# Norm factors of both layers loaded ahead of layer 0, and keys of two latent heads made by one matmul

## The chip, the core and the metric

The kernel runs on one core of a Trainium2 chip. Five engines work side by side on it, each with its own instruction stream that it works off in order: TensorE (PE in the profile; its weight loads are PEld), VectorE (DVE), ScalarE (ACT), GpSimd (POOL) and SyncE (SP), which here only issues DMAs. The metric is the time of one execution on the device in microseconds, as a median of several runs.

## The reference

Two layers of an encoder over 512 tokens of width 1024. Each layer projects its input once, and three kinds of attention share the result: six latent heads (A), six dilated heads (B) and four grouped-query heads over two key heads (C). Then come an output projection, a normalisation, a SwiGLU network of width 2816 and another normalisation. What the change touches are A's keys and values and C's norm factors:

```python
for l in range(DEPTH):                       # DEPTH = 2
    h = x @ w_in[l]
    ckv = rms_norm(h[..., 256:384], mla_kv_norm[l])
    # A: 128 latent values of a token give 6 heads x (64 key + 64 value) columns
    kva = (ckv @ mla_w_ukv[l]).reshape(B, S, 6, 64 + 64)
    ka = concatenate([kva[..., :64], rope(k_rope) broadcast to 6 heads])
    va = kva[..., 64:]
    out_a = dense_attention(qa, ka, va, 96 ** -0.5)
    out_b = dilated_mixture(...)
    # C: 4 query heads and 2 key heads of 64, each normalised and rotated
    qc = rms_norm(qc, gqa_q_norm[l]);  kc = rms_norm(kc, gqa_k_norm[l])
    out_c = dense_attention(axial_rope(qc), axial_rope(kc), vc, 64 ** -0.5)
    x = layer_norm(ALPHA * x + concatenate([out_a, out_b, out_c]) @ w_out[l])
    x = layer_norm(ALPHA * x + (silu(x @ w_gate[l]) * (x @ w_up[l])) @ w_down[l])
```

All inputs are float32; `gqa_q_norm` and `gqa_k_norm` are vectors of 64 values for each layer.

## The kernel before

**Numbers.** Every float32 operand of a projection is split into a high and a low part, and a product is made by three matmuls: high by high, high by low, low by high (`mm3`, L162 to L167; in the profile they are L165, L166 and L167). A weight is brought in by `wload` (L142 to L157): SP issues a DMA into a raw buffer (L150; two such buffers take turns), ScalarE copies it rounded into `whi` (L152), and VectorE or GpSimd subtracts to get `wlo` (L156).

**Order of the work.** A layer first projects the values of the dilated heads and then runs its 16 attention heads one after another in units of one head and one tile of 128 queries (`attend`): scores (L241), the row's minimum and the exponential, the reciprocal of the sum (L255), the scaling of the row by it on GpSimd (`pl`, L256), transposition on TensorE (`ptr`, L264) with the split into PTh and PTl (L271, L272), and the product with the values (`po`, L282 and L283), three and four units later. Six dilated heads come first, then four grouped-query heads, then six latent heads. The other projections of the layer are cut into steps that a table of units (`W`, L33) spreads between the attention units, so that TensorE has work while a softmax runs. A scheduler finally orders the instructions of every engine when the kernel is built, by its own estimate of times; on the chip each engine works its list off in order. After attention come the rest of the output projection, the normalisation and the feed-forward network, which fill more than half of the time.

**Grouped-query norm factors.** At each layer's head a tile `gg` of 128 partitions by 6 heads by 64 is filled by six DMAs (L406), four of `gqa_q_norm` and two of `gqa_k_norm`; each repeats one vector of 64 on all partitions. VectorE then scales the first four by -1/8 (L407). `gg` has one buffer, so layer 1's loads can't start before layer 0 has used it for the last time (L426 in `evac_g2`).

**Latent heads.** `latent_qv` loads the two halves of `w_uq` and `w_ukv` as whole rows of 768 columns, in the order head, key or value, column; it makes the queries (`uq`) and, with the value columns of all heads as a moving operand of 384 columns, the values (`uv`). `mla_T(h)` runs once a head, at the units that `W['mT']` names: it transposes the queries (`tT`), and makes the keys by one `mm3` with 64 columns of weights and 512 tokens as moving operand (`kT`, 64 partitions of a PSUM bank). ScalarE and VectorE write the high and low part into a tile of the head, whose partitions 64 to 95 get the rotated keys by a DMA. These tiles share four buffers with the queries; the `kT`, `uv`, `uq` and projection products share two PSUM banks (`ps_mm`).

Of the kernel before, what the change touches and what calls it, by code (L numbers as in the profile page):

```python
# [10 lines left out]
F32 = mybir.dt.float32  # L11
F32R = mybir.dt.float32r
AF = mybir.ActivationFunctionType
ALU = mybir.AluOpType
# [67 lines left out]
def encoder(ctx: ExitStack, tc, x, w_in, mla_q_norm, mla_kv_norm, w_uq, w_ukv, gqa_q_norm, gqa_k_norm, rel_bias,  # L82
# [30 lines left out]
    def bank(pl, name):  # L113
        return pl.tile([P, 512], F32, tag="b", name=name)
# [24 lines left out]
             "m": ((pmix, "m"), (pmix, "m"))}  # L139
    turn = {"raw": 0}  # L140

    def wload(src, shape, lo, ring="w", raw="w"):  # L142

        n = shape[1] * shape[2]
        if raw == "wd":
            turn["raw"] += 1
            raw = "wwdd"[turn["raw"] % 4]
        (hp, ht), (lp, lt) = parts[ring]
        r = raws[raw][0].tile([P, 1024], F32, tag=raws[raw][1], name="wraw")
        nc.sync.dma_start(r[:, :n].rearrange("p (a c) -> p a c", a=shape[1]), src)  # L150
        h = hp.tile([P, 1024], F32R, tag=ht, name="whi")
        A.copy(h[:, :n], r[:, :n])  # L152
        o = lp.tile([P, 1024], F32R, tag=lt, name="wlo")
        step = n // 2 if lo is G and SPLIT else n
        for c in range(0, n, step):
            lo.tensor_tensor(o[:, c:c + step], r[:, c:c + step], h[:, c:c + step].bitcast(F32), op=ALU.subtract)  # L156
        return (h[:, :n].rearrange("p (a c) -> p a c", a=shape[1]), o[:, :n].rearrange("p (a c) -> p a c", a=shape[1]))  # L157

    def krows(w, k0, nk, c0, c1):
        return w[k0 * P:(k0 + nk) * P, c0:c1].rearrange("(k p) c -> p k c", p=P)  # L160
# [232 lines left out]
    for l in range(DEPTH):  # L393
# [3 lines left out]
        if l == 0:  # L397
            nc.sync.dma_start(tab[:, P:], tabs[:, P:])
            for i in range(DEPTH):
                nc.sync.dma_start(gm[:, i, 0:2], mla_q_norm[i].rearrange("(k p) -> p k", p=P))  # L400
                nc.sync.dma_start(gm[:, i, 2:3], mla_kv_norm[i].rearrange("(k p) -> p k", p=P))

        gg = pgg.tile([P, 6, HD], F32, tag="gg", name="gg")
        for i in range(6):
            src = (gqa_q_norm if i < 4 else gqa_k_norm)[l]
            nc.sync.dma_start(gg[:, i], src.unsqueeze(0).to_broadcast([P, HD]))  # L406
        V.tensor_scalar(gg[:, 0:4], gg[:, 0:4], -(HD ** -0.5), None, op0=ALU.mult)  # L407

        g2, gv, gkk = {}, {}, []

# [112 lines left out]
        def mla_T(h):  # L523
            assert ("q", h // 3) in told
            to_T(lambda t: tq[0][:, t, h, :], 96, mqk[h])
            yield
            pb = bank(ps_mm, "kT")
            wk = [w[:, 0, h * P:h * P + HD] for w in wkv[0]]
            r = pqk.tile([P, 2, T], F32R, tag="q", name="kT")
            nc.sync.dma_start(r[HD:96].bitcast(F32), krT[0][:32].bitcast(F32))  # L530
            mm3(pb[:HD], wk, (latT[2][:, 0], latT[2][:, 1]), True, True)
            A.copy(r[:HD, 0], pb[:HD])
            V.tensor_tensor(r[:HD, 1], pb[:HD], r[:HD, 0].bitcast(F32), op=ALU.subtract)
            mqk[h].append(r)
            yield

        def dil_qk(pair):
# [36 lines left out]
        def latent_qv():  # L574
            q = pxt.tile([P, NT, 6, 96], F32, tag="x", name="tq")
            tq.append(q)
            wq = [wload(krows(w_uq[l], 0, 2, 288 * c, 288 * c + 288), (P, 2, 288), LO['uq']) for c in range(2)]
            wkv.append(wload(krows(w_ukv[l], 0, 1, 0, 768), (P, 1, 768), LO['kv']))
            yield
            for c in range(2):  # L580
                h, o = wq[c]
                for t in range(NT):
                    pb = bank(ps_mm, "uq")[:, :288]
                    ts = slice(t * P, (t + 1) * P)
                    for k in range(2):
                        mm3(pb, (latT[k][:, 0, ts], latT[k][:, 1, ts]), (h[:, k], o[:, k]), k == 0, k == 1)
                    A.copy(q[:, t, 3 * c:3 * c + 3, :], pb.rearrange("p (h c) -> p h c", h=3))
                    yield
                tm = ppl.tile([P, T], F32, tag="l", name="qrt")[:, :384].rearrange("p (t h c) -> p t h c", t=NT, h=3)
                rope32(q[:, :, 3 * c:3 * c + 3, 64:96], 3, tm)  # L590
                told.append(("q", c))
            h, o = (w[:, 0].rearrange("p (h c) -> p h c", h=6)[:, :, HD:] for w in wkv[0])
            for t in range(NT):
                pb = bank(ps_mm, "uv")[:, :6 * HD]
                ts = slice(t * P, (t + 1) * P)
                mm3(pb, (latT[2][:, 0, ts], latT[2][:, 1, ts]), (h, o), True, True)
                vt = pv_sb.tile([P, 6, 2, HD], F32R, tag="v", name="mv")
                split_v(vt, pb.rearrange("p (a c) -> p a c", a=6))
                mv_.append(vt)
                yield  # L600
# [53 lines left out]


        latT, krT, tq, mv_, wkv, dts, told = [], [], [], [], [], {}, []
        gqk, dqk, mqk = ([[] for _ in range(n)] for n in (2, 3, 6))
        heads = []
        for h in range(6):
# [205 lines left out]
```

## Time and profile before

| | before |
|---|---|
| median of three runs | 1281.85 us (1281.53 to 1283.26) |
| profiled execution, its own time | 1282.31 us |
| its span, first to last instruction | 1280.5 us |
| TensorE busy | 98% of the span |
| VectorE / ScalarE / GpSimd busy | 54% / 42% / 25% |
| mean granted clock of TensorE | 0.994 |
| mean DMA traffic | 96 GB/s |

A row of the timeline gives the start of an instruction, how long it took, the engine, the line of the kernel, the operation, the tile written, the tiles read and the shape. In square brackets stands how long the engine had been idle before it and what ended that. Matmuls are pipelined, so the distance of two starts tells more of TensorE than the length of one. The granted clock is a share of TensorE's full speed: 1.00 is 2.4 GHz, 0.50 is 1.2 GHz.

### The profile page before, as it was taken

How to read it: one execution, taken by the hardware profiler on the slowest of the kernel's cores; microseconds unless marked ns; L12 is line 12 of the kernel's file. 1: busy time of each engine (PE TensorE's matmuls, PEld its weight loads, DVE VectorE, ACT ScalarE, POOL GpSimd, SP SyncE). 2: the span in 40 equal slices, each digit the busy share in tenths (PEclk: the TensorE clock that was granted, in tenths of full speed). 3: DMA queues.
4: the chain of work that ended last, by engine and by line, in shares of the span. 5: the costliest groups of instructions: out<-in, count | busy, mean ns of one | idle time of the engine just before them, and what ended most of it. 6: DMA issues, size and time to landing. Idle time of an engine off the chain costs nothing.

```text
span 1280.5 us, 16743 instructions
## 1 busy us (share of the span) xinstructions
PE 1250.1 (98%) x6352; PEld 1062.5 (83%) x6352; DVE 687.7 (54%) x1138; ACT 543.6 (42%) x955; POOL 324.6 (25%) x344
## 2 busy tenths in 40 slices
PE   8999899999999999999999998999999999999997
PEld 7888788889888888888898897888988888888885
DVE  4377997684333333332664889966843332333346
ACT  4465786544222212222245668855342221222222
POOL 0445475661000000000245456655500000000004
PEclk9999899999999999999999999999999999999999
DMA  5623210324333233332425231114243333333223
GB/s 179 188 67 87 87 34 13 120 69 130 99 99 97 89 96 98 99 99 99 148 78 147 84 103 48 28 30 134 77 115 99 99 99 99 99 99 98 92 96 110
DMA packets 140552, 122.57 MB, mean 96 GB/s; under 512 B 6924, under 2 KB 114572, under 8 KB 140472
## 3 DMA queue, kind: packets, MB, share of 16 engines
q1 hardware_dynamic: 140460, 121.48, 32.0%
q8 instruction: 50, 0.82, 0.3%
q14 instruction: 30, 0.25, 0.1%
q10 hardware_dynamic: 12, 0.02, 0.0%
HBM read 114.65 MB, written 2.12 MB: 91 GB/s over the span
## 4 chain that ended last, share of the span: by engine, by line
PE 80%; DVE 8%; DMA 4%; ACT 3%; POOL 2%; issue 2%; SPq 0%; DVEq 0%; POOLq 0%; ACTq 0%
PE gate L165 6%; PE down L167 6%; PE down L166 6%; PE up L167 6%; PE down L165 6%; PE up L165 6%; PE up L166 6%; PE gate L167 6%; PE gate L166 6%; PE sc L241 4%; PE ptr L264 3%; PE po L283 2%; PE po L282 2%; PE tp L166 1%; PE tp L165 1%
## 5 line engine op out<-in xcount | busy, mean ns | idle before, releaser
L152 ACT CAST whi<-wraw 128x1024 fp32r<-128x1024 f32 (+3 forms) x202 | 205.6, 1020 | 550.6 <-PE gate L166 149.3
L156 DVE TENSOR_TENSOR wlo<-wraw,whi 128x1024 fp32r<-128x1024 f32 (+3 forms) x170 | 208.2, 1226 | 319.7 <-ACT whi L152 315.7
L191 POOL TENSOR_TENSOR rstd<-mv,eps_l 128x1 f32<-128x1 f32 x16 | 5.7, 357 | 680.8 <-DVE mv L200 680.8
L256 POOL TENSOR_TENSOR pl<-pl,srec 128x512 f32<-128x512 f32 x128 | 135.7, 1061 | 153.0 <-DVE srec L255 139.2
L166 PE MATMUL gate<-xTl,whi 128*128 128x512 f32 (+1 forms) x384 | 142.8, 372 | 0.0
L166 PE MATMUL up<-xTl,whi 128*128 128x512 f32 (+1 forms) x384 | 142.7, 372 | 0.0
L167 PE MATMUL gate<-xTh,wlo 128*128 128x512 f32 (+1 forms) x384 | 142.7, 372 | 0.0
L167 PE MATMUL up<-xTh,wlo 128*128 128x512 f32 (+1 forms) x384 | 142.7, 372 | 0.0
L165 PE MATMUL up<-xTh,whi 128*128 128x512 f32 (+1 forms) x384 | 142.6, 372 | 0.0
L165 PE MATMUL gate<-xTh,whi 128*128 128x512 f32 (+1 forms) x384 | 142.4, 371 | 0.0
L167 PE MATMUL down<-whi,act 128*128 128x512 f32 x352 | 136.7, 389 | 0.0
L166 PE MATMUL down<-wlo,act 128*128 128x512 f32 x352 | 136.7, 389 | 0.0
L165 PE MATMUL down<-whi,act 128*128 128x512 f32 x352 | 136.7, 389 | 0.0
L779 DVE TENSOR_TENSOR sg<-sg,up 128x512 f32<-128x512 f32 x44 | 30.3, 688 | 136.1 <-PE up L167 134.8
L156 POOL TENSOR_TENSOR wlo<-wraw,whi 128x512 fp32r<-128x512 f32 (+2 forms) x64 | 79.4, 1265 | 78.7 <-ACT whi L152 78.4
L272 DVE TENSOR_TENSOR PTl<-ptr,PTh 128x512 fp32r<-128x512 f32 x128 | 87.2, 682 | 8.7 <-ACT PTh L271 7.6
L271 ACT CAST PTh<-ptr 128x512 fp32r<-128x512 f32 x128 | 74.9, 586 | 38.9 <-PE ptr L264 38.4
L167 PEld LDWEIGHTS up<-xTh,wlo 128*128 128x128 f32 x384 | 72.4, 189 | 12.6
L165 PEld LDWEIGHTS gate<-xTh,whi 128*128 128x128 f32 x384 | 72.3, 188 | 12.5
L166 PEld LDWEIGHTS up<-xTl,whi 128*128 128x128 f32 x384 | 72.3, 188 | 12.5
L166 PEld LDWEIGHTS gate<-xTl,whi 128*128 128x128 f32 x384 | 72.4, 188 | 12.4
L165 PEld LDWEIGHTS up<-xTh,whi 128*128 128x128 f32 x384 | 72.3, 188 | 12.4
(174 smaller groups left out, 2493.6 us busy)
## 6 DMA issues: line engine op xcount, KB each, us to landing
wraw<-in_ffn_w_down SPq DMA_DIRECT2D x54, 512.0 KB, 3.6
wraw<-in_ffn_w_up SPq DMA_DIRECT2D x44, 512.0 KB, 3.9
wraw<-in_ffn_w_gate SPq DMA_DIRECT2D x44, 512.0 KB, 3.9
wraw<-in_w_in SPq DMA_DIRECT2D x20, 512.0 KB, 4.7
wraw<-in_w_out SPq DMA_DIRECT2D x14, 512.0 KB, 3.7
dt<-tdr SPq DMA_DIRECT2D x12, 448.0 KB, 3.9
wraw<-in_w_in SPq DMA_DIRECT2D x8, 416.0 KB, 3.4
wraw<-in_w_in SPq DMA_DIRECT2D x8, 384.0 KB, 3.9
```

The lines of the kernel that those rows point to most:

```text
L152: A.copy(h[:, :n], r[:, :n])
L156: lo.tensor_tensor(o[:, c:c + step], r[:, c:c + step], h[:, c:c + step].bitcast(F32), op=ALU.subtract)
L165: TE.matmul(ps, ah, bh, start=first, stop=False)
L166: TE.matmul(ps, ah, bl, start=False, stop=False)
L167: TE.matmul(ps, al, bh, start=False, stop=last)
L241: TE.matmul(sc, a, b, start=i == 0, stop=i == len(ops) - 1)
L256: G.tensor_tensor(pl, pl, r.to_broadcast([P, T]), op=ALU.mult)
L264: TE.transpose(pb[:, kt * P:(kt + 1) * P], pl[:, kt * P:(kt + 1) * P], ident)
L271: A.copy(ph[:, :, c:c + P], pb)
L272: V.tensor_tensor(plo[:, :, c:c + P], pb, ph[:, :, c:c + P].bitcast(F32), op=ALU.subtract)
L282: TE.matmul(po[:, h0:h0 + 256], self.vst(kt), ph[:, kt], start=kt == 0, stop=False)
L779: V.tensor_tensor(sg, sg, pss[1], op=ALU.mult)
```

## The change

Three things differ, and nothing of what is computed.

The norm factors of both layers are loaded in layer 0's start into one tile of 128 x 2 x 6 x 64, by four DMAs in place of two times six: for each layer one whose source repeats the query vector four times, and one that repeats the key vector twice. One instruction of VectorE scales both layers.

The keys of the latent heads h and h + 1 (h even) are made by one `mm3` with 128 columns of weights. The two halves of the PSUM bank are written apart into the tiles of the two heads, when the keys of the even head are made; for the odd head only the queries are transposed.

So that the weights of two heads stand side by side, `w_ukv` is loaded by two DMAs into the two halves of the raw buffer: first the key columns of all heads, then the value columns. Each reads six runs of 64 columns (256 bytes) for each of 128 partitions. The cast and the subtraction cover both halves at once, as before, and `uv` now takes its 384 columns in one piece.

```diff
-    def wload(src, shape, lo, ring="w", raw="w"):
+    def wload(src, shape, lo, ring="w", raw="w", by=1):
...
-        nc.sync.dma_start(r[:, :n].rearrange("p (a c) -> p a c", a=shape[1]), src)
+        for i in range(by):
+
+            d = r[:, i * n // by:(i + 1) * n // by]
+            nc.sync.dma_start(d.rearrange("p (a c) -> p a c", a=shape[1] // by) if by == 1 else
+                              d.rearrange("p (a c) -> p a c", c=src[i].shape[-1]), src if by == 1 else src[i])
...
-        gg = pgg.tile([P, 6, HD], F32, tag="gg", name="gg")
-        for i in range(6):
-            src = (gqa_q_norm if i < 4 else gqa_k_norm)[l]
-            nc.sync.dma_start(gg[:, i], src.unsqueeze(0).to_broadcast([P, HD]))
-        V.tensor_scalar(gg[:, 0:4], gg[:, 0:4], -(HD ** -0.5), None, op0=ALU.mult)
+        if l == 0:
+
+            gga = pgg.tile([P, DEPTH, 6, HD], F32, tag="gg", name="gg")
+            for j in range(DEPTH):
+                for src, a, b in ((gqa_q_norm, 0, 4), (gqa_k_norm, 4, 6)):
+                    nc.sync.dma_start(gga[:, j, a:b], src[j].unsqueeze(0).unsqueeze(0).to_broadcast([P, b - a, HD]))
+            V.tensor_scalar(gga[:, :, 0:4], gga[:, :, 0:4], -(HD ** -0.5), None, op0=ALU.mult)
+        gg = gga[:, l]
...
         def mla_T(h):
             to_T(lambda t: tq[0][:, t, h, :], 96, mqk[h])
             yield
-            pb = bank(ps_mm, "kT")
-            wk = [w[:, 0, h * P:h * P + HD] for w in wkv[0]]
-            r = pqk.tile([P, 2, T], F32R, tag="q", name="kT")
-            nc.sync.dma_start(r[HD:96].bitcast(F32), krT[0][:32].bitcast(F32))
-            mm3(pb[:HD], wk, (latT[2][:, 0], latT[2][:, 1]), True, True)
-            A.copy(r[:HD, 0], pb[:HD])
-            V.tensor_tensor(r[:HD, 1], pb[:HD], r[:HD, 0].bitcast(F32), op=ALU.subtract)
-            mqk[h].append(r)
+            if h % 2 == 0:
+
+                kT = bank(ps_mm, "kT")
+                wk = [w[:, 0, h * HD:(h + 2) * HD] for w in wkv[0]]
+                mm3(kT, wk, (latT[2][:, 0], latT[2][:, 1]), True, True)
+                for e in range(2):
+                    pb = kT[64 * e:64 * e + 64]
+                    r = pqk.tile([P, 2, T], F32R, tag="q", name="kT")
+                    nc.sync.dma_start(r[HD:96].bitcast(F32), krT[0][:32].bitcast(F32))
+                    A.copy(r[:HD, 0], pb)
+                    V.tensor_tensor(r[:HD, 1], pb, r[:HD, 0].bitcast(F32), op=ALU.subtract)
+                    mlk[h + e] = r
+                    if e == 0:
+                        mqk[h].append(r)
+            else:
+                mqk[h].append(mlk[h])
             yield
...
-            wkv.append(wload(krows(w_ukv[l], 0, 1, 0, 768), (P, 1, 768), LO['kv']))
+            wkv.append(wload([w_ukv[l].rearrange("p (h s c) -> p s h c", h=6, s=2)[:, i] for i in range(2)], (P, 2, 384), LO['kv'], by=2))
...
-            h, o = (w[:, 0].rearrange("p (h c) -> p h c", h=6)[:, :, HD:] for w in wkv[0])
+            h, o = (w[:, 1] for w in wkv[0])
```

The diff moves instructions at several places, since the order of each engine is decided anew. Three of them matter here. In the rows, a line number of after is four to sixteen higher than that of before for the same statement.

The first place is VectorE in layer 0's attention, among the dilated heads: `sc` are scores, `pl` the row of probabilities, `nm` its minimum, `g` and `rt` belong to the rotation of a grouped-query tile, `krt` to that of the latent key. Before:

```order
L247 ISA pl,nm<-sc,dt 128x512
L247 ISA nm 128x1
L442 TENSOR_TENSOR g_1123<-rt,g_1123 128x4x64
L407 TENSOR_SCALAR gg<-gg 128x256
L255 RECIPROCAL srec<-ssum 128x1
L474 TENSOR_TENSOR krt<-g_1241,tab 128x16
```

After:

```order
L251 ISA pl,nm<-sc,dt 128x512
L251 ISA nm 128x1
L448 TENSOR_TENSOR g_1121<-rt,g_1121 128x4x64
L259 RECIPROCAL srec<-ssum 128x1
L480 TENSOR_TENSOR krt<-g_1239,tab 128x16
```

The scaling of layer 1's factors is gone from this place, and with it the loads that it waited for; the rest stands in the same order.

The second place is VectorE at the start of the kernel: `xTl` are the low parts of the transposed input, two instructions for a block of 128 tokens, `wlo` those of the four parts of the first weight. Before:

```order
L181 TENSOR_TENSOR xTl<-xtr,xTh 128x512 x3
L407 TENSOR_SCALAR gg<-gg 128x256
L156 TENSOR_TENSOR wlo<-wraw,whi 128x768 x2
L181 TENSOR_TENSOR xTl<-xtr,xTh 128x512 x3
L366 TENSOR_TENSOR dv<-tp,dv 128x6x64 x3
```

After:

```order
L185 TENSOR_TENSOR xTl<-xtr,xTh 128x512 x3
L160 TENSOR_TENSOR wlo<-wraw,whi 128x768
L412 TENSOR_SCALAR gg<-gg 128x2x256
L185 TENSOR_TENSOR xTl<-xtr,xTh 128x512 x2
L160 TENSOR_TENSOR wlo<-wraw,whi 128x768
L185 TENSOR_TENSOR xTl<-xtr,xTh 128x512
```

The scaling has moved behind the third `wlo`, and the fourth `wlo` behind two more instructions for `xTl`. SP's order there changes with it: before, one load of factors stands ahead of the third part of the weight, four between it and the fourth, one behind; after, one ahead of the third part, and three loads of factors and that of `rel_bias` between it and the fourth. The new loads ahead of the fourth part are of four, two, four and two repeats.

The third place is TensorE in layer 0, where the keys of the fifth latent head are made: `mv` are the values, `tT` transposed queries of the next head, `opp` the output projection of the other heads. Before:

```order
L264 MATMUL ptr<-tab,pl 128x128 x4
L165 MATMUL kT<-lat,whi 64x512
L166 MATMUL kT<-lat,whi 64x512
L167 MATMUL kT<-lat,wlo 64x512
L241 MATMUL sc<-kT,qkT 128x512 x3
L504 MATMUL tT<-tab,tq 96x128 x4
L264 MATMUL ptr<-tab,pl 128x128 x4
...
L264 MATMUL ptr<-tab,pl 128x128 x4
L165 MATMUL opp<-whi,mix 128x512
```

After:

```order
L268 MATMUL ptr<-tab,pl 128x128 x4
L169 MATMUL kT<-lat,whi 128x512
L170 MATMUL kT<-lat,whi 128x512
L171 MATMUL kT<-lat,wlo 128x512
L245 MATMUL sc<-kT,qkT 128x512 x3
L510 MATMUL tT<-tab,tq 96x128 x4
L268 MATMUL ptr<-tab,pl 128x128 x4
...
L268 MATMUL ptr<-tab,pl 128x128 x4
L245 MATMUL sc<-kT,qkT 128x512 x6
```

The group of three has 128 rows of result instead of 64, and in place of the next head's group, which came later, there is none. Behind it the output projection has moved back: the scores of two units now follow on each other without it.

## Rows read from the trace of the kernel before

**Rows 1.** The page: busy microseconds, share and instructions of TensorE; granted clock by slice
```profile
PE 1250.1 (98%) x6352; PEld 1062.5 (83%) x6352; DVE 687.7 (54%) x1138; ACT 543.6 (42%) x955; POOL 324.6 (25%) x344
...
PEclk9999899999999999999999999999999999999999
```

**Rows 2.** The page: shares of the chain that ended last
```profile
PE 80%; DVE 8%; DMA 4%; ACT 3%; POOL 2%; issue 2%; SPq 0%; DVEq 0%; POOLq 0%; ACTq 0%
```

**Rows 3.** Waits of TensorE, whole span: waiter, releaser: total us, times, longest us
```profile
PE po L283 <- DVE PTl L272: 7.1, 6, 2.3
...
PE ptr L264 <- POOL pl L256: 2.7, 3, 2.2
...
PE tp L166 <- DVE wlo L156: 1.0, 1, 1.0
```

**Rows 4.** Timeline of VectorE in layer 0, 117.9 to 124.6 us (start, length, engine, ...)
```profile
118.42 0.65 DVE L442 TENSOR_TENSOR g<-rt,g 128x256 f32<-128x256 f32 x1
124.34 0.29 DVE L407 TENSOR_SCALAR gg<-gg 128x256 f32<-128x256 f32 x1 [5.27 <-DMA gg<-in_gqa_q_norm]
```

**Rows 5.** Timeline of TensorE in layer 0, 120 to 132 us
```profile
120.93 0.48 PE L241 MATMUL sc<-dk,dqk 128*128 128x512 f32 x1
...
125.87 0.33 PE L264 MATMUL ptr<-tab,pl 128*128 128x128 f32 x1 [2.21 <-POOL pl L256]
...
127.78 0.73 PE L241 MATMUL sc<-dk,dqk 128*128 128x512 f32 x1 [0.87 <-DVE nm L247]
...
131.53 0.39 PE L241 MATMUL sc<-dk,dqk 128*128 128x512 f32 x1
```

**Rows 6.** Timeline of TensorE in layer 1, the same instructions
```profile
753.53 0.48 PE L241 MATMUL sc<-dk,dqk 128*128 128x512 f32 x1
...
759.00 0.40 PE L241 MATMUL sc<-dk,dqk 128*128 128x512 f32 x1
```

**Rows 7.** Windows: us, busy of PE, PEld, DVE, ACT, POOL; clock, DMA share, GB/s
```profile
127.50:131.50 4.00, 3.72 (x11) 3.42 (x12) 3.26 (x12) 3.27 (x8) 2.41 (x3) 0.57 0.01 2
184.00:192.00 8.00, 7.88 (x51) 6.51 (x50) 8.00 (x17) 6.06 (x13) 3.70 (x4) 1.00 0.01 2
192.00:204.00 12.00, 12.00 (x80) 10.54 (x81) 11.26 (x24) 10.80 (x26) 7.45 (x7) 1.00 0.10 23
...
220.00:236.00 16.00, 16.00 (x92) 13.72 (x92) 10.72 (x25) 9.56 (x21) 10.35 (x11) 1.00 0.12 37
```

**Rows 8.** Timelines of VectorE and of TensorE at the start, 14 to 20 us
```profile
18.56 0.29 DVE L407 TENSOR_SCALAR gg<-gg 128x256 f32<-128x256 f32 x1 [3.54 <-DMA gg<-in_gqa_q_norm]
18.77 0.95 DVE L156 TENSOR_TENSOR wlo<-wraw,whi 128x768 fp32r<-128x768 f32 x1
...
19.77 0.45 PE L166 MATMUL tp<-wlo,xTh 128*128 128x384 f32 x1 [1.00 <-DVE wlo L156]
```

**Rows 9.** Timeline of ScalarE at the start
```profile
20.21 0.83 ACT L152 CAST whi<-wraw 128x768 fp32r<-128x768 f32 x1 [4.91 <-DMA wraw<-in_w_in]
```

**Rows 10.** The tile kT, both layers (mean, median, longest ns), and TensorE's timeline, layer 0
```profile
L165 PE MATMUL kT<-lat,whi x12: 393/477/478, 180.4 to 856.1; 128*64 128x512 f32 x12
...
228.62 0.48 PE L165 MATMUL kT<-lat,whi 128*64 128x512 f32 x1
...
229.39 0.87 PE L241 MATMUL sc<-kT,qkT 96*128 96x512 f32 x3
```

**Rows 11.** Timelines of ScalarE and of TensorE in layer 1, 755 to 775 us
```profile
763.09 0.84 ACT L152 CAST whi<-wraw 128x768 fp32r<-128x768 f32 x1 [0.66 <-DMA wraw<-in_mla_w_ukv]
...
772.98 0.58 PE L283 MATMUL po<-PTl,dv 128*128 128x256 f32 x1 [2.31 <-DVE PTl L272]
```

**Rows 12.** DMA issues from 755 to 770 us: count, KB, us from issue to landing
```profile
wraw<-in_mla_w_ukv SPq DMA_DIRECT2D x1, 384.0 KB, 3.3
```

**Rows 13.** DMA queue: packets, MB, share; 115.5 to 119.4 us, then 21 to 22.5 us
```profile
q1 hardware_dynamic: 292, 0.07, 6.8%
...
q1 hardware_dynamic: 714, 0.37, 95.4%
```

More of the change, by code (lines that the diff above doesn't have):

```diff
@@ L656, in encoder @@
         latT, krT, tq, mv_, wkv, dts, told = [], [], [], [], [], {}, []
+        mlk = {}
         gqk, dqk, mqk = ([[] for _ in range(n)] for n in (2, 3, 6))
```

## The prediction

> **What bounds the kernel now.** I read the page first: busy shares, then the forty slices, then the chain. TensorE is busy 98% of the span, its granted clock 9 tenths or more in all slices but one [rows 1], and it holds 80% of the chain, VectorE 8%, DMA 4% [rows 2]. So time can come from two places only: instructions that TensorE no longer runs, and the few stretches where it waits. The waits of TensorE come next: 7.1 us in six waits for PTl, 2.7 us in three for pl, 1.0 us once for wlo [rows 3]. Last I read the timelines around those waits, engine by engine, which tell why the engine named was late.
>
> The largest cause stands on VectorE in layer 0. It ends an instruction that starts at 118.42 us, and then waits 5.27 us for the norm factors of layer 1 (L407); they are scaled by an instruction of 0.29 us [rows 4]. Everything behind it in VectorE's order waits too: the reciprocals that POOL needs for pl, the minima that ScalarE needs. TensorE goes on with projections for a while and then idles 2.21 and 0.87 us [rows 5]. After that the granted clock is 0.57 over 127.5 to 131.5 us, so for most of it at 1.2 GHz instead of 2.4 [rows 7].
>
> **Part 1: the factors of layer 1 leave layer 0's attention.** Layer 1 runs the same instructions in the same order without this wait, so it serves as a control inside the same trace. From the score matmul that starts at 120.93 us to the one at 131.53 us layer 0 takes 10.60 us [rows 5]; the same two in layer 1 lie at 753.53 and 759.00 us, 5.47 us apart [rows 6]. The difference, 5.13 us, is what the wait costs with its idle time and its slow clock. After the change layer 0 holds no load and no scaling there, and the order behind is that of layer 1: **-5.1 us** (4.5 to 5.3). What is late next is what is late in layer 1, and the 5.47 us hold it already.
>
> **Part 2: the start.** All factors are now loaded and scaled there. Before, the scaling stands ahead of the third wlo: VectorE idles 3.54 us for the factors, starts wlo at 18.77 us, and TensorE waits 1.00 us for it [rows 8]. Now the third wlo comes first, and the scaling holds only xTl of the third token block and what follows, which TensorE reaches some 14 matmuls later. The scaling has twice the elements (from 0.29 us to about twice that, an estimate from its row), beside TensorE's projections. SP issues four loads of factors where it issued six; behind them stands the fourth weight load, for which ScalarE waited 4.91 us until 20.21 us [rows 9]. TensorE now needs that weight after the rest of the third one, so it may come as late as before. **-1.0 us**, with 0 and -1.3 as ends: 0 if the fourth load sets the pace, -1.3 if it lands a little earlier too.
>
> **Part 3: keys of two latent heads by one matmul.** Before there are 12 groups of three matmuls, one for each head and layer [rows 10]. One group takes 229.39 - 228.62 = 0.77 us of TensorE's order [rows 10]. Half of them go: three in each layer, 2.3 us. The product now fills 128 columns of the array instead of 64, but streams the same 512 columns; ScalarE and VectorE still make the two halves one by one, as many instructions as before. So VectorE's work is unchanged, and where VectorE is the bound, nothing is won. From 184 to 192 us VectorE is busy 8.00 of 8.00 us, from 192 to 204 us 11.26 of 12.00; from 220 to 236 us only 10.72 of 16.00 [rows 7]. The keys of heads 1 and 3 lie in the first two stretches: the two groups (1.54 us) can give no more than VectorE's idle 0.74 us; I take half, 0.4. Head 5's keys lie in the third: up to 0.77. But there the new order runs four rounds of scores without an output-projection matmul between them, so some of it becomes waiting; I take 0.5. Per layer 0.9, for both **-1.8 us**. The ends are -3.0 (all of 0.74 and 0.77, twice) and +1.7: the product's bank and the second head's buffer come free only when older scores are done, the third uv product waits for that, and a pause there of the size of rows 5 could bring another fall of the clock, which by part 1 costs 5.13 - 2.21 - 0.87 = 2.05 us together with small waits.
>
> **Part 4: the w_ukv load in two parts.** To put the keys of two heads side by side, each load now fetches 256-byte runs, in two DMAs behind each other on SP, where one DMA fetched whole rows. This one has a waiter: in layer 1 ScalarE already idles 0.66 us for it and starts the cast at 763.09 us [rows 11], and behind the cast in ScalarE's order stand an exponential, the copy of the latents and more, for which VectorE waits in turn. TensorE idles 2.31 us for that VectorE chain at 772.98 us [rows 11], so a later landing goes through nearly in full. Now that layer 0 runs like layer 1, both pay. Lower end: the second DMA is issued 0.4 us later and lands 0.4 us later. Upper end: the whole load takes 3.3 us from issue to landing [rows 12]; if the second part starts when the first is done and takes as long, 3.3 us. The nearest rows for how loads share a queue are the old factor loads: 292 short packets in 3.9 us, at 6.8% of the engines, so about 75 packets a microsecond with the engines nearly idle; one load of 128 packets every 1.7 us [rows 13]. Something in the queue serves such loads one after another. The weight load with eight runs a partition reaches 714 packets in 1.5 us [rows 13], so it isn't the packet that costs. A part that occupies the queue for 1.7 us would delay the second landing by 1.7 us. I take 1.3, between 0.4 and 1.7 and nearer the row: **+2.6 us** for two layers (0.8 to 6.6).
>
> **Sum:** -5.1 - 1.0 - 1.8 + 2.6 = -5.3 us. The profiled execution took 1282.31 us with a span of 1280.5 us; so 1277.0 us by its own time. The median of the runs shown is 1281.85 us, 0.46 below it: **1276.5 us**. The ends of the parts, not all at once: 1273.5 to 1279.5.
>
> **Rivals.**
>
> *The split load costs almost nothing* (its lower end, 0.8 us in all): 1276.5 - 1.8 = 1274.7 us. For it: 714 packets in 1.5 us show that many runs can be served quickly. Against: one load every 1.7 us in the other row.
>
> *The keys give nothing*: VectorE bounds heads 1 and 3 fully, and the missing projections around head 5 leave TensorE waiting: 1278.3 us. For it: 8.00 of 8.00 us. Against: TensorE is busy 16.00 of 16.00 us in the stretch of head 5.
>
> *The two parts land one after the other, 3.3 us later in each layer*, since short runs are slow as well: +6.6 instead of +2.6, 1280.5 us, no change. For it: ScalarE's wait is there already. Against: the share of rows 13 gives 0.068 x 16 x 3.9 / 292 = 14.5 ns of an engine for a short packet and 0.954 x 16 x 1.5 / 714 = 32 ns for a 512-byte one, so a short packet is not dearer by the byte. The Trainium skill, "DMA: Bandwidth & Descriptors", section Specifications, speaks for this rival: it says that a transfer needs at least 512 bytes for line rate, since the engine reads, modifies and writes below this. By that rule the 256-byte runs would pay again; the trace does not agree, since half the bytes took less than half the time.
>
> *Slower: the factor loads choke the start.* The place is SP's queue before the third and fourth weight loads. The factors are read with a source that repeats for every partition, and if the 75 packets a microsecond are a rate per packet of such loads, not per load, the new DMAs (512, 256, 512 and 256 packets) take 20 us. The fourth weight load stood behind 640 such packets and now behind 1536: 896 / 75 = 11.9 us later. It decides from about 1 us of delay, since TensorE has no other work then. Of 11.9 us some 11 stay: -5.3 + 1.0 + 11, plus the slow clock afterwards, 1288 to 1290 us. Against it: the eight-run load of rows 13, which is six times faster by the packet.
>
> **How the numbers follow.** Forecast 0.60; cheap split load 0.12; no gain from keys 0.12; parts in series 0.10; choked start 0.06. A change under 0.2% (2.6 us) can't be told from none here, so "same" is 1279.3 to 1284.4 us. Faster: 0.56 of the forecast's 0.60, 0.12, and 0.10 of the third case: 0.78. Same: the 0.04 and 0.02 left, and 0.10: 0.16. Slower: 0.06. The range leaves out the choked start, half of the series case and a little below: 1272.5 to 1280.6 us.
>
> **What would show it.** Part 1: no L407-like wait on VectorE near 118 us, and the two score matmuls about 5.5 us apart in both layers. Part 2: no wait of tp for wlo before 20 us, and projections done about 1 us earlier. Part 3: six groups of kT in place of 12, VectorE still full from 184 to 200 us. Part 4: ScalarE's idle time before the 128x768 cast grows from 0.66 us to about 2 us in both layers, and the 2.31 us wait for PTl grows with it. I am wrong if the distance of the two score matmuls in layer 0 stays above 8 us, if that cast waits over 4 us, or if TensorE stands still for several microseconds before 35 us.

## The result, and the profile after

The changed kernel takes 1290.85 us (median of 4 runs, 1287.12 to 1291.45), the kernel before, measured beside it, 1282.55 us. The ratio is 1.0059 (95% interval 1.0038 to 1.0080): 0.6% slower, where 0.4% faster was forecast. The profiled execution took 1291.09 us with a span of 1289.3 us, 8.8 us more than that of before.

The page of the changed kernel, busy time and granted clock as in [rows 1]:

```profile
PE 1253.7 (97%) x6334; PEld 1064.7 (83%) x6334; DVE 694.7 (54%) x1137; ACT 545.9 (42%) x955; POOL 325.1 (25%) x344
...
PEclk8999899999999999999999999999999999999999
```

TensorE runs 18 matmuls fewer and is still busy 3.6 us longer: part of the loss is a slow clock. The first slice is new among those under 9. Its waits, whole span, as in [rows 3]:

```profile
PE po L287 <- DVE PTl L276: 6.2, 4, 2.3
...
PE po L286 <- ACT PTh L275: 3.9, 4, 2.5
PE xtr L181 <- DVE xTl L185: 2.0, 1, 2.0
PE tT L524 <- ACT g L470: 1.8, 2, 0.9
PE tp L169 <- ACT whi L156: 1.6, 1, 1.6
```

The 2.7 us for pl are gone from the head of the list; the last four rows are new or grown, and each belongs to another place of the kernel.

To find the places, each matmul of TensorE was matched with the same one of the other trace (same statement, same tiles, same count), and the difference of the two starts was taken; both traces are of one execution. Its median over 10 us of the trace of before says how late the changed kernel is there:

| stage (us of the trace before) | late at its end | gained in the stage |
|---|---|---|
| start, 20 to 30 | +7.0 | +7.0 |
| dilated heads of layer 0, 120 to 131 | +1.8 | -5.1 |
| behind the w_ukv load, layer 0, 139 to 152 | +3.7 | +1.9 |
| latent heads to the feed-forward, layer 0, 180 to 310 | +4.2 | +0.5 |
| feed-forward of layer 0, start of layer 1, 310 to 760 | +4.2 | 0.0 |
| behind the w_ukv load, layer 1, 760 to 790 | +4.9 | +0.7 |
| latent heads of layer 1, 800 to 880 | +4.9 | 0.0 |
| end of layer 1's attention, 885 to 910 | +8.6 | +3.7 |
| the rest | +8.5 | -0.1 |

**The start.** First ScalarE's cast of the third weight, in the kernel before and in the changed one:

```profile
14.47 0.83 ACT L152 CAST whi<-wraw 128x768 fp32r<-128x768 f32 x1 [0.18 <-DMA wraw<-in_w_in]
```

```profile
18.93 0.83 ACT L156 CAST whi<-wraw 128x768 fp32r<-128x768 f32 x1 [4.81 <-DMA wraw<-in_w_in]
```

Then, of the changed kernel, the cast of the fourth weight, VectorE and TensorE (each row from its engine's timeline), and two windows, 21.7 to 31.9 and 31.9 to 42 us, with the columns of [rows 7]:

```profile
26.91 0.83 ACT L156 CAST whi<-wraw 128x768 fp32r<-128x768 f32 x1 [6.17 <-DMA wraw<-in_w_in]
...
25.22 0.43 DVE L412 TENSOR_SCALAR gg<-gg 128x512 f32<-128x512 f32 x1 [4.46 <-DMA gg<-in_gqa_q_norm]
...
19.82 0.62 PE L169 MATMUL tp<-whi,xTh 128*128 128x384 f32 x2 [1.57 <-ACT whi L156]
...
26.30 1.11 PE L181 MATMUL xtr<-tab,xtok 128*128 128x128 f32 x4 [1.98 <-DVE xTl L185]
...
21.70:31.90 10.20, 8.22 (x28) 7.71 (x27) 3.60 (x6) 1.80 (x3) 0.00 (x0) 0.50 0.67 164
31.90:42.00 10.10, 10.07 (x48) 7.79 (x48) 5.43 (x8) 4.45 (x6) 0.00 (x0) 1.00 0.41 105
```

The third weight is cast 4.5 us later than before, the fourth at 26.91 us instead of 20.21 [rows 9]. So TensorE stands still again where [rows 8] has its 1.00 us: 1.57 and 0.37 us, now for the third weight itself. VectorE waits for the factors 4.46 us in front of xTl, for which TensorE waits 1.98 us. And the granted clock is 0.50, that is 1.2 GHz, for 10.2 us: it falls at 21.7 us, after the first two of these waits, and stays low across the one that ends at 26.30; before, there is none of it here. What the DMA queue does then (the issues between 11.4 and 24.9 us), and two issues from SP's timeline:

```profile
wraw<-in_w_in SPq DMA_DIRECT2D x1, 384.0 KB, 10.3
gg<-in_gqa_k_norm SPq DMA_DIRECT2D x2, 64.0 KB, 9.0
gg<-in_gqa_q_norm SPq DMA_DIRECT2D x1, 128.0 KB, 12.8
...
12.26 3.15 SPq L411 DMA_DIRECT2D gg<-in_gqa_q_norm  x1
...
16.58 0.38 SPq L153 DMA_DIRECT2D wraw<-in_w_in  x1
```

A load of 64 KB takes 9.0 us, one of 128 KB 12.8 us, and the weight behind them 10.3 us. In the records of the single packets the 1536 packets of 256 bytes run from 11.41 to 24.88 us: 114 a microsecond. The fourth weight's load is also issued late, at 16.58 us instead of 14.40, since SP stands 3.15 us on one factor load before it: 2.2 of its 6.7 us.

**The dilated heads.** The two score matmuls of [rows 5] now lie 5.47 us apart, to the hundredth as far as those of layer 1 [rows 6]:

```profile
127.86 0.48 PE L245 MATMUL sc<-dk,dqk 128*128 128x512 f32 x1
...
133.33 0.39 PE L245 MATMUL sc<-dk,dqk 128*128 128x512 f32 x1
```

**The w_ukv load.** Timelines of ScalarE (layer 0, layer 1) and of TensorE (layer 0), then the window 148 to 154.8 us:

```profile
138.78 0.83 ACT L156 CAST whi<-wraw 128x768 fp32r<-128x768 f32 x1 [1.87 <-DMA wraw<-in_mla_w_ukv]
...
768.50 0.84 ACT L156 CAST whi<-wraw 128x768 fp32r<-128x768 f32 x1 [1.98 <-DMA wraw<-in_mla_w_ukv]
...
142.87 0.66 PE L524 MATMUL tT<-tab,g 128*128 128x128 f32 x4 [0.92 <-ACT g L470]
...
148.64 0.58 PE L287 MATMUL po<-PTl,dv 128*128 128x256 f32 x1 [2.31 <-DVE PTl L276]
...
148.00:154.80 6.80, 6.16 (x26) 5.76 (x27) 5.82 (x14) 2.23 (x6) 1.84 (x3) 0.50 0.29 97
```

In layer 1 ScalarE's wait has grown from 0.66 [rows 11] to 1.98 us, 1.32 us more. TensorE pays with a new wait for tT, not with the one for PTl, which is 2.31 us as before; and in layer 0 the slow clock behind it lasts 6.8 us, where it lasted 3.5 (144.9 to 148.4 us).

**The latent heads.** Windows of layer 0, shifted by how late the kernel is there, to hold about the same work as those of [rows 7]:

```profile
187.70:195.70 8.00, 7.68 (x49) 6.22 (x49) 7.94 (x16) 5.70 (x13) 2.91 (x4) 1.00 0.01 2
195.70:207.70 12.00, 11.28 (x72) 9.37 (x71) 11.09 (x23) 10.79 (x24) 8.20 (x8) 1.00 0.10 23
...
224.20:240.20 16.00, 15.69 (x88) 12.79 (x86) 11.14 (x25) 11.11 (x24) 12.52 (x12) 1.00 0.20 62
```

VectorE is as full as before in the first two, and TensorE, which was busy 12.00 of 12.00 us in the second, is so for 11.28: the matmuls that went have left idle time.

**The end of layer 1's attention.** Timelines of ScalarE and TensorE, then the window 902.3 to 905.7 us:

```profile
897.47 1.05 ACT L156 CAST whi<-wraw 128x1024 fp32r<-128x1024 f32 x1 [1.22 <-DMA wraw<-in_ffn_w_up]
898.42 0.58 ACT L275 CAST PTh<-ptr 128x512 fp32r<-128x512 f32 x1
899.02 0.37 ACT L292 COPY pvt<-po 64x256 f32<-64x256 f32 x1
899.29 1.04 ACT L156 CAST whi<-wraw 128x1024 fp32r<-128x1024 f32 x1
900.36 0.59 ACT L275 CAST PTh<-ptr 128x512 fp32r<-128x512 f32 x1
...
901.00 0.39 PE L286 MATMUL po<-PTh,mv 128*128 128x256 f32 x1 [2.55 <-ACT PTh L275]
...
902.30:905.70 3.40, 3.40 (x10) 2.67 (x9) 2.06 (x6) 0.00 (x0) 1.76 (x4) 0.50 0.69 197
```

The split of the last probabilities stands in ScalarE's order behind casts of the first feed-forward weights, and one of these waits for its load. TensorE has nothing else, idles 2.55 us, and runs at 1.2 GHz for 3.4 us after. In the kernel before, the second of these casts finds its weight there, and TensorE waits 0.21 us at this matmul (ScalarE, then TensorE):

```profile
889.51 1.05 ACT L152 CAST whi<-wraw 128x1024 fp32r<-128x1024 f32 x1
...
893.53 0.38 PE L282 MATMUL po<-PTh,mv 128*128 128x256 f32 x1 [0.21 <-ACT PTh L271]
```

### The profile page after: what moved, and what is told of

It is laid out like the page before. It is cut to its first block, busy times and chain, and to the rows that moved or that the text cites. A ratio compares the mean times of both kernels' runs of the same rounds, so it can differ in the third digit from the quotient of the medians.

```text
span 1289.3 us, 16692 instructions
## 1 busy us (share of the span) xinstructions
PE 1253.7 (97%) x6334; PEld 1064.7 (83%) x6334; DVE 694.7 (54%) x1137; ACT 545.9 (42%) x955; POOL 325.1 (25%) x344
## 4 chain that ended last, share of the span: by engine, by line
PE 81%; DVE 7%; ACT 4%; DMA 4%; issue 2%; POOL 1%; SPq 0%; DVEq 0%; POOLq 0%; ACTq 0%
PE gate L170 6%; PE up L170 6%; PE up L171 6%; PE gate L171 6%; PE gate L169 6%; PE up L169 6%; PE down L170 6%; PE down L171 6%; PE down L169 6%; PE sc L245 4%; PE ptr L268 3%; PE tp L169 2%; PE tp L170 2%; PE tp L171 2%; PE po L287 2%
## 5 line engine op out<-in xcount | busy, mean ns | idle before, releaser
L276 DVE TENSOR_TENSOR PTl<-ptr,PTh 128x512 fp32r<-128x512 f32 x128 | 87.7, 685 | 12.8 <-ACT PTh L275 10.8
L171 PEld LDWEIGHTS gate<-xTh,wlo 128*128 128x128 f32 x384 | 72.3, 188 | 12.4
```

Source lines behind the costliest of these rows:

```text
L171: TE.matmul(ps, al, bh, start=False, stop=last)
L276: V.tensor_tensor(plo[:, :, c:c + P], pb, ph[:, :, c:c + P].bitcast(F32), op=ALU.subtract)
```

## Experiments

All times are medians, beside the kernel before on the same chip (1281.1 to 1281.5 us).

**The two halves of the change.** gg_only is the kernel before with the new factor loads alone; keys_only has the paired keys and the w_ukv load in two parts alone.

> Only the factor loads are changed (both layers' factors by four loads at the start), keys and w_ukv as before. Theory A (the changed kernel's start is late because packets that all read the same few bytes go at about 100 a microsecond, 1536 of them instead of 768): start later by about 7.0 us, layer 0's attention shorter by 5.1 us, nothing else: +1.9 us against before, about 1284.4 us; 256-byte packets end near 25 us again. Rival B (the late start comes with the other parts of the change): start as before or 1 us earlier, about 1276.5 us.

> Only the paired keys and the w_ukv load in two parts; factor loads as before. If the parts add up: +1.9 us in layer 0 around 140 us (w_ukv lands 1.3 us later, longer slow clock), +0.6 us in its latent heads, +0.7 us in layer 1 around 767 us, +3.7 us at the end of layer 1's attention: +6.9 us, about 1289.4 us, TensorE waiting 2.5 us for PTh near 895 us. Rival: the wait at the end of layer 1's attention belongs to the order that came with the factor loads: +3.2 us, about 1285.7 us. By the prediction's terms it would have been -1.8 + 2.6 = +0.8 us.

gg_only: 1282.14 us, ratio 1.0005 (0.9996 to 1.0014): 0.6 us slower where theory A had 1.9; rival B falls. The matched matmuls are 5.6 us late after the start and 5.1 us from 60 us on, and 5.1 us are won back near 130 us. So in this one execution the start is 1.4 to 1.9 us cheaper than in the full change. Its fourth weight is cast 0.8 us earlier; TensorE idles about as long in all (0.57, 0.38 and 3.26 us against 1.57, 0.37 and 1.98), but the clock falls only after the last of these waits, and the slow stretch lasts 3.4 us (from 26.3 us) instead of 10.2 (from 21.7 us). ScalarE, then TensorE:

```profile
26.13 0.83 ACT L152 CAST whi<-wraw 128x768 fp32r<-128x768 f32 x1 [5.89 <-DMA wraw<-in_w_in]
...
25.93 0.83 PE L177 MATMUL xtr<-tab,xtok 128*128 128x128 f32 x4 [3.26 <-DVE xTl L181]
```

keys_only: 1289.50 us, ratio 1.0062 (1.0049 to 1.0075), 8 us slower, more than the 6.9 of the parts. TensorE waits 2.84 us for PTh at the end of layer 1's attention, so that wait belongs to the keys or their load. In the execution traced, 1.4 us of the 8 are lost between 40 and 60 us, ahead of everything that this half changes. The two halves give 0.6 + 8.0 = 8.6 us; the whole change 8.3.

```profile
902.13 0.39 PE L286 MATMUL po<-PTh,mv 128*128 128x256 f32 x1 [2.84 <-ACT PTh L275]
```

**What is slow in the factor loads.** gg_apart and gg_apart2 issue the same loads as gg_only, but each partition reads bytes of its own:

```diff
-  src[j].unsqueeze(0).unsqueeze(0).to_broadcast([P, b - a, HD])
+  w_in[j, 0:P, a * HD:b * HD].rearrange("p (i c) -> p i c", c=HD)                    # gg_apart
+  w_in[j, 0:P, a * P:b * P].rearrange("p (i s c) -> p i s c", s=2, c=HD)[:, :, 0]    # gg_apart2
```

> As gg_only, with as many loads, packets and bytes in the same order of SP, but each partition reads its own bytes (rows of w_in, so the factors are wrong and the output differs from the reference in the grouped-query heads). Theory A (same bytes read by all partitions are slow): the 1536 packets take a few microseconds, the fourth weight load is no later than before, -5.1 to -6.1 us, 1276.4 to 1277.4 us. Rival C (256-byte packets are slow whatever they read): as gg_only, start 7 us later, about 1284.4 us.

> As gg_only in every instruction's place, with the same 1536 packets of 256 bytes, but each partition reads its own bytes (every second 64 columns of rows of w_in, so the factors are wrong and the grouped-query heads differ from the reference). In gg_apart the bytes of a partition lay side by side and went as fewer, longer packets, so it did not tell the two apart. Theory A (slow is that all partitions read the same bytes): packets at several hundred a microsecond, start not late, 1276 to 1277.5 us. Rival C (slow is the number of 256-byte packets): start about 5 us late as in gg_only, about 1282 us.

gg_apart: 1276.10 us, 0.9961 (0.9948 to 0.9975). It doesn't tell the theories apart: the bytes of a partition are contiguous there, and went as 1 KB and 512-byte packets. gg_apart2 keeps the packets at 256 bytes: 1275.60 us, 0.9957 (0.9944 to 0.9970). Its loads (11 to 20 us) and the cast of the fourth weight:

```profile
gg<-in_w_in SPq DMA_DIRECT2D x2, 64.0 KB, 2.9
gg<-in_w_in SPq DMA_DIRECT2D x1, 128.0 KB, 2.4
...
18.05 0.83 ACT L152 CAST whi<-wraw 128x768 fp32r<-128x768 f32 x1 [0.17 <-DMA wraw<-in_w_in]
```

As many packets of the same size, in the same place of SP's order: 2.4 and 2.9 us in place of the 12.3 and 8.9 of gg_only. The packets run from 11.24 to 15.13 us, 395 a microsecond. So neither their size nor their number is slow, but the source that repeats for all partitions. Whether it is that the same bytes are read, or that the access pattern has a step of zero, no run tells apart. The third weight is cast at 14.79 us here, at 18.43 in gg_only, and TensorE, with both weights in time, is 0.7 us earlier than in the kernel before at 30 us and 1.2 us at 60.

**Fewer such packets.** gg_rows loads both layers' vectors as one run of 512 bytes for each partition (256 packets instead of 1536) and lets VectorE expand them:

```diff
+            gga = pgg.tile([P, 6, DEPTH, HD], F32, tag="gg", name="gg")
+            for i, src in ((0, gqa_q_norm), (4, gqa_k_norm)):
+                nc.sync.dma_start(gga[:, i], src.unsqueeze(0).to_broadcast([P, DEPTH, HD]))
+            V.tensor_scalar(gga[:, 1:4], gga[:, 0:1].to_broadcast([P, 3, DEPTH, HD]), -(HD ** -0.5), None, op0=ALU.mult)
+            V.tensor_scalar(gga[:, 0], gga[:, 0], -(HD ** -0.5), None, op0=ALU.mult)
+            V.tensor_copy(gga[:, 5], gga[:, 4])
```

> Factors of both layers by two loads at the start, 128 partitions reading the same 512 bytes each (256 packets), expanded to six heads by three instructions of VectorE; keys and w_ukv as before. Theory A: about 2.5 us of such packets instead of 8, start 0 to 2 us earlier than before, layer 0's attention 5.1 us shorter: 1275.4 to 1277.4 us. Rival D (the time of such packets goes by bytes, 128 KB instead of 192 KB before): start about as before, 1277.4 us, packets end near 17 us. Rival B' (any load ahead of the weight costs its issue and its landing): not earlier than 1277.4 us.

1275.44 us, ratio 0.9953 (0.9941 to 0.9966): the fastest of all, though gg_apart and gg_apart2, which load other values in place of the factors, lie within 0.7 us of it. The 256 packets run from 11.29 to 13.90 us, 98 a microsecond. These packets hold twice the bytes of those of before (94 a microsecond in its start) and go at a like rate, so the time goes by the packet; rivals D and B' fall. The fourth weight is cast at 16.94 us, 3.3 us earlier than before, and the key factors land 3.2 us after their issue. Of the earlier weight little reaches TensorE (0.3 us at 30 us): the gain is the 5 us of the dilated heads, and 1.3 us more that come in small steps near 300 and 770 us, which the traces of gg_only and gg_apart2 have as well.

```profile
16.94 0.83 ACT L152 CAST whi<-wraw 128x768 fp32r<-128x768 f32 x1 [0.96 <-DMA wraw<-in_w_in]
```

**The load without the pairs, the pairs without the load.** split_only has w_ukv in two parts, but makes each head's keys alone, from `w[:, 0, h * HD:(h + 1) * HD]`; TensorE and ScalarE have the order of before. keys_whole loads whole rows by one DMA, and the cast and the subtraction sort them:

```diff
+            rs = r[:, :n].rearrange("p (h s c) -> p s h c", h=6, s=2)
+            A.copy(h[:, :n].rearrange("p (s h c) -> p s h c", h=6, s=2), rs)
```

> Only the w_ukv load in two parts; keys one head at a time, TensorE and ScalarE in the order of the kernel before. Theory (the second part lands 1.3 us later and ScalarE passes that on): +1.2 us in layer 0 near 140 us, +1.0 us in layer 1 near 767 us, no wait at the end of layer 1's attention: about +2.2 us, 1283.7 us. Rival (the late load also pushes the end of the attention): about +5 us, with TensorE waiting over 2 us for PTh near 890 us.

> Paired keys, but w_ukv comes as whole rows in one DMA and the cast and the subtraction sort the columns; factor loads as before; TensorE and ScalarE in the order of keys_only. Theory (what is lost at the end of the attention comes from the order with paired keys, not from the load): ScalarE waits 0.6 us for w_ukv as before, so 2.2 us better than keys_only, but the wait of about 2.5 us near 890 us stays: about 1285 to 1287 us. Rival (all the loss comes from the load): 1279.7 us, the 1.8 us that the prediction gave for the keys.

split_only: 1283.81 us, ratio 1.0021 (1.0012 to 1.0029), +2.6 us. ScalarE waits 1.47 and 1.70 us (0.55 and 0.66 before), and there is no new wait near 890 us. SP takes 1.32 us to issue the two parts of layer 1, where the one load took it 0.35 us. Their landing, then ScalarE in both layers:

```profile
wraw<-in_mla_w_ukv SPq DMA_DIRECT2D x2, 192.0 KB, 3.2
...
136.06 0.83 ACT L156 CAST whi<-wraw 128x768 fp32r<-128x768 f32 x1 [1.47 <-DMA wraw<-in_mla_w_ukv]
...
764.41 0.83 ACT L156 CAST whi<-wraw 128x768 fp32r<-128x768 f32 x1 [1.70 <-DMA wraw<-in_mla_w_ukv]
```

keys_whole: 1285.44 us, ratio 1.0033 (1.0021 to 1.0045). ScalarE waits 0.61 us as before, and TensorE still waits at the end. The pairs alone cost 4.2 us where -1.8 was forecast.

```profile
762.67 0.84 ACT L155 CAST whi<-wraw 128x768 fp32r<-128x768 f32 x1 [0.61 <-DMA wraw<-in_mla_w_ukv]
...
895.51 0.38 PE L290 MATMUL po<-PTh,mv 128*128 128x256 f32 x1 [2.55 <-ACT PTh L279]
```

**Which pair.** pair0123 is keys_whole with the keys of heads 4 and 5 made one by one, pair45 with those of heads 0 to 3 (`if h in LONE:` takes the old code of `mla_T`). From the 57th unit of a layer to the end of its attention ScalarE has the order of before in the first, and that of keys_whole in the second.

> As keys_whole (w_ukv as whole rows, factor loads as before), but only heads 0 to 3 are paired; heads 4 and 5 get their keys one by one, and from there to the end of the attention ScalarE has the order of the kernel before. Theory (the end of the attention is late because of the order that the pair of heads 4 and 5 brings; the first two pairs save nothing since VectorE sets the pace there): no wait over 1 us near 890 us, -0.5 to +0.5 us against before. Prediction's term: 0.4 us in each layer, -0.8 us. Rival (every pair gives its 0.77 us): -3.1 us. Rival (the wait near 890 us comes from any pairing): +3 us or more.

> As keys_whole, but only heads 4 and 5 are paired; from their keys on ScalarE has the order of keys_whole. Theory (that pair's order delays the end of the attention): TensorE waits about 2.5 us for PTh near 890 us, +3 to +4.5 us, as keys_whole. Rival (it is the first pairs): no such wait, and -1.5 to 0 us.

pair0123: 1282.90 us, ratio 1.0010 (1.0001 to 1.0019). No wait at the end, and a loss of 1.8 us (0.1 to 2.4 by the interval), where the theory had 0.5 at most: the matched matmuls lose 0.7 us between 180 and 310 us, and 0.6 between 790 and 900. Between 160 and 310 us the kT matmuls take 1.50 us less of TensorE's order, po 1.29 more, sc 0.72 more and tT 0.49 more (distances of starts, summed by tile). pair45: 1284.09 us, ratio 1.0020 (1.0011 to 1.0029). Its pair gives 0.7 us near 220 us, but 0.6 of them are gone near 230, where the projection that has moved back stands, and from 210 to 310 us only 0.2 stay, no more than gg_only shows there with nothing changed (0.4). Summed by tile as above, the kT matmuls take 0.75 us less, sc 0.53, op 0.35 and po 0.26 more. At the end of layer 1 it loses 3.2 us (from -1.85 to +1.37 between 880 and 890 us), and the slow clock behind takes another 0.9. TensorE at the same matmul, pair0123 and then pair45:

```profile
894.06 0.38 PE L291 MATMUL po<-PTh,mv 128*128 128x256 f32 x1 [0.21 <-ACT PTh L280]
```

```profile
894.57 0.39 PE L291 MATMUL po<-PTh,mv 128*128 128x256 f32 x1 [2.80 <-ACT PTh L280]
```

**An attempt to mend the end.** whole_op64 is keys_whole with `op=(51, 64)` for `op=(51, 65)`.

> As keys_whole, with one entry of the table of units changed: the output projection of the other heads is to end one unit earlier, (51, 64) for (51, 65). The last two casts of w_out then stand behind the same exponential as in the kernel before, not one later. Theory (the projection moved back, its weight buffers came free late, the first feed-forward weights landed late): the wait near 890 us goes, 3 us better than keys_whole, 1280 to 1283 us. Rival (the wait comes from the early second half of the keys or from VectorE): unchanged against keys_whole.

1287.70 us, ratio 1.0050 (1.0036 to 1.0063): 2.3 us slower than keys_whole where 3 us faster was expected, so the theory failed. The last two casts of w_out do come 1.2 us earlier (881.68 us), and ScalarE's wait for the weight of `up` falls from 1.26 to 0.29 us. But TensorE still idles 0.56 and 1.57 us, then 2.6 us for xTl among the first feed-forward matmuls, and the slow clock lasts 6.9 us.

```profile
890.58 0.63 PE L272 MATMUL ptr<-tab,pl 128*128 128x128 f32 x4 [0.56 <-DVE PTl L280]
...
892.78 0.58 PE L290 MATMUL po<-PTh,mv 128*128 128x256 f32 x1 [1.57 <-ACT PTh L279]
```

That the pair of heads 4 and 5 brings the wait is shown; that it is the place of the projection's buffers is not. Which of the moved instructions decides stays open.

**Together.** rows_pair0123 joins gg_rows and pair0123.

> gg_rows (factors of both layers by two loads of 128 partitions by 512 bytes) together with pair0123. If the parts add up, -6 us from the factors and what pair0123 gives: 1275 to 1276 us by the theory, 1274.6 us by the prediction's term for the keys. Rival: the earlier start is lost again in another order, over 1277 us.

1277.31 us, ratio 0.9964 (0.9950 to 0.9977), over 1277 us as the rival had it: no gain over gg_rows, whose interval this one overlaps. The parts as measured add up (-6.1 + 1.8 = -4.3 us, measured -3.8). The first two pairs may as well be left out.

## Why the prediction was wrong

**Part 1 was right, to the tenth.** -5.1 us were forecast from layer 1 as a control; 5.1 us were won, in the full change as in gg_only, and the distance of the two matmuls is that of layer 1.

**Part 2 failed, and it is the largest error.** The step was "so it may come as late as before", with 0 and -1.3 as ends: measured +7.0. The fourth weight came 6.7 us later. The third, whose wait of 1.00 us the term let go, was 4.5 us late too, since 512 packets of factors stood ahead of it instead of 128. With a source of its own for each partition (gg_apart2) the forecast -1.0 came about, 0.7 to 1.2 us: the order was read rightly, and the time of the loads was missed. Its price was in the text, as the rival of the choked start, and its rate too: 75 packets a microsecond [rows 13], 114 now. It got a chance of 0.06 because the weight load of [rows 13] is six times faster by the packet. But those packets read each their own bytes, as gg_apart2's do; of the rows of [rows 13] only the first has the same source for all partitions, and that one was slow. The fast row was no evidence against it. The rival's 11.9 us became 6.7 us at the cast, since 896 packets more take 7.9 us at 114 a microsecond (an estimate), and the slow clock added what it did not count. The 7.0 us come out of two parts: TensorE idles 2.9 us more than before, and half of the 8.22 us that it is busy in the slow stretch, 4.1 us, is put down to the clock (an estimate: half the clock, twice the time). That the rival's 1288 to 1290 us lie near the result is partly chance: the next term has its share in them.

**Part 3 failed twice.** -1.8 us were forecast. For heads 0 to 3 the rival "the keys give nothing" came nearest: po, sc and tT wait for what the kT matmuls save and 1 us beyond, and VectorE stays as full as before. That the two halves' subtractions, which now follow on each other, make it so is argued and not shown. For heads 4 and 5 0.5 us a layer were forecast, and nothing clear of the other runs stayed (0.2 us in layer 0 of pair45). What was missed is the end of layer 1's attention, 30 us behind: what ScalarE does next comes in another order there, and the prediction, which named waiting only round the keys ("some of it becomes waiting"), doesn't look at the place. The upper end, +1.7 for both layers, was set at the keys' own place (how it follows from the 2.05 us beside it isn't worked out); at the end of layer 1 alone +3.7 us came.

**Part 4 was right in its size, and partly by luck.** +2.6 us were forecast, split_only measured +2.6 (1.5 to 3.7). ScalarE's wait grew by 1.3 us in the full change and by 0.9 and 1.0 in split_only. But the 1.3 us were chosen near 1.7, the time of a factor load, whose slowness comes from its repeated source; these loads have none. What the runs show for it is SP's issue, 1.3 us for two parts in place of 0.35 for one, so 1.0 us more where the lower end had 0.4. The path was another in part: not a longer wait for PTl, which stayed 2.31 us, but one for tT, and more slow clock in layer 0. Both parts are issued within 1.3 us in split_only's layer 1 and land 3.2 us after, the whole load 3.3 us before [rows 12]: they don't follow one another, so the rival of parts in series (+6.6) falls. It leaned on the rule of the Trainium skill, "DMA: Bandwidth & Descriptors", section Specifications, that transfers under 512 bytes miss line rate; the 256-byte packets of gg_apart2, 128 KB in 2.4 us, show no such cost that would decide here. The prediction's own argument against it doesn't hold, though: its 32 ns are a mean with some long packets in it. By the median the 512-byte packets of that row took 27 ns, its 256-byte packets 15 ns and those of w_ukv in two parts 18, so half the bytes took more than half the time.

**The sum** of the measured stages: -5.1 + 7.0 + 1.9 + 0.7 (both w_ukv places) + 0.5 + 3.7 = 8.7 us, of the 8.8 us between the spans.

## What to carry to other kernels

A load that repeats one short source on all partitions is paid by the packet, at 75 to 114 a microsecond here, where packets with a source of their own went at 395; load each vector once for a partition in the longest run there is, and expand it on chip. To take such loads out of the queue ahead of the first weights stands to reason, but no run tried it. Before a row is used against a rival, ask whether it differs from the rival in the one thing that the rival is about. And where a tuned order is decided anew, look at the last place before the next stage, where no filler is left: removing 0.75 us of matmuls cost some 3 us there.

## What was not expected of the hardware

The packets of the shared source run at 94 a microsecond in the start of the kernel before (768 in 8.2 us) and at 114 in that of the changed one, while the engines show 6.8% busy in such a stretch [rows 13]: the queue looks idle while it is the bottleneck. 6.8% of 16 engines is 1.1 engines, so about one packet was in work at a time (an estimate from that row).

At the start the 1.2 GHz lasted 3.4 us in gg_only and 10.2 us in the full change, with nearly the same idle time in all (4.2 and 3.9 us). The two differ in where the idle time lies: in the full change the clock fell after waits of 1.57 and 0.37 us and stayed low across the last one, in gg_only the first wait was 0.57 us and the clock fell after the last. What decides that, one execution of each doesn't show.
